# The adaLN sums over rows: 32x32 block transposes and additions on VectorE, and a fold of 8 columns on TensorE

## The chip, the cores and the metric

One core of a Trainium2 chip runs the whole program. The time is that of the device for one execution, in microseconds; the core has TensorE (matrix products), VectorE, ScalarE and GpSimd (work on rows), and DMA queues that bring the weights from HBM.

## The reference

Two layers of a transformer trunk over 256 latent and 256 context tokens with 1024 features. Each layer is a half-step FFN, a mixing stage and a second half-step FFN; the norm ahead of each, and the result of each, are modulated by nine vectors of 1024 values. These come from the conditioning vectors `c` and `c_ctx` through one matrix per layer:

```python
def modulate(h, shift, scale):
    return h * (1 + scale) + shift

def ffn_half_step(h, shift, scale, gate, g, w_in, w_out):
    a, b = jnp.split(modulate(rms_norm(h, g), shift, scale) @ w_in, 2, axis=-1)
    return h + FFN_RESIDUAL_WEIGHT * gate * ((jax.nn.silu(a) * b) @ w_out)
...
    sc, scc = jax.nn.silu(c), jax.nn.silu(c_ctx)
    for l in range(DEPTH):
        mod_l = jnp.split((sc @ w_ada[l] + b_ada[l])[:, None, :], ADA_CHUNKS, axis=-1)
        mod_c = jnp.split((scc @ w_ada[l] + b_ada[l])[None, None, :], ADA_CHUNKS, axis=-1)
        h = ffn_half_step(h, mod_l[0], mod_l[1], mod_l[2], g_ffn1[l], w_ffn1_in[l], w_ffn1_out[l])
        hc = ffn_half_step(hc, mod_c[0], mod_c[1], mod_c[2], g_ffn1[l], w_ffn1_in[l], w_ffn1_out[l])
```

The change concerns only the product `sc @ w_ada[l]` and its twin for the context: two vectors of 1024 times a 1024 x 9216 matrix, per layer.

## The kernel before

The stream `h` lies feature by feature: 8 blocks of 128 features on the partitions, 512 tokens in the columns. Weights come as tiles `raw` of 128 x 1024 through SyncE's DMA queue, in the order of use, six tiles ahead (class `Weights`). ScalarE copies each into a high part `whi` (L125), VectorE (or GpSimd) takes the rest as a low part `wlo` (L126), five weights ahead of their use; both are written into the buffer of a weight that TensorE has finished. A product of 128 x 128 weights with 512 tokens is three matmuls, high by high, high by low and low by high (L384 to L386).

The work is a list of jobs, emitted one after the other; each engine keeps its instructions in the order of emission. An FFN has 22 pairs of blocks: `pair_a` and `pair_b` are 24 matmuls each, after which `evac` forms silu(a) times b (ScalarE L452, VectorE L453, ScalarE L454, VectorE L455). Then come 8 output blocks of three jobs (8, 8 and 6 blocks of 128 features, three matmuls each, 66 in all).

The adaLN products are spread between these jobs. `ada_job` puts one tile of `w_ada` (256 rows by 512 columns of one of the chunks) after a job: in the first FFN after both jobs of each of its 19 later pairs and after two jobs of each of the first five output blocks, in the two FFNs around the layers' boundary less densely. VectorE multiplies its rows by the two conditioning values of each partition and adds them up in `scratch`, four instructions of 128 x 512 per tile (L276 for the first two of a sum, L278 otherwise). Four tiles (part 0 to 3) make one sum, half a chunk: 512 columns for two streams, with 128 partial sums each, one per partition. `scratch` is one buffer of 128 x 1024.

The addition over the partitions then goes through TensorE. `pend` is a list of emissions with a count of ordinary jobs by which they come later. `ada_sum` (count 2) multiplies the four quarters of `scratch` by ones, each into another group of 32 rows of a PSUM bank `sm` (L288, two passes each); ScalarE copies the result (L291). `ada_finish` (count 1, from there) transposes it back on TensorE, so that features lie on partitions (L297), and VectorE adds the bias (L304). `sm` has two buffers.

Of the kernel before, what the change touches and what calls it, by code (L numbers as in the profile page):

```python
# [8 lines left out]
F32 = mybir.dt.float32  # L9
# [6 lines left out]
L = 2  # L16
# [23 lines left out]
# packed per-partition parameters: name -> columns for one layer  # L40
# [20 lines left out]
class Weights:  # L61
    """Streams weights in order: DRAM -> raw tile -> (high, low) float32r parts, ahead of their use.
    SPARE in the stream is room of one weight, left to other uses between its take and its done."""
# [29 lines left out]
    def pump(self, preps=None):  # L93
        """Start the loads that have room, and prepare the parts (at most preps, when held back)."""
        nc = self.nc
        go = True
        left = preps if preps is not None else (0 if self.hold else 1 << 30)
        while go:
            go = False
            while self.dma_i < len(self.raws) and self.dma_i < self.raw_pref + RAWB:  # L100
                raw = self.raws[self.dma_i]
                t = self.pool.tile([128, RAWN], F32, tag="raw", name="raw", bufs=RAWB)
                nc.sync.dma_start(out=t[:, 0:raw["n"]], in_=raw["ap"])
                self.raw_t[self.dma_i] = t
                self.dma_i += 1
                go = True
            while left > 0 and self.prep_i < len(self.subs) and self.prep_i < self.sub_pref + SUBB:
                if self.subs[self.prep_i] is None:
                    self.sub_t[self.prep_i] = self._parts(F32)
                    self.prep_i += 1  # L110
                    left -= 1
                    continue
                r, (off, n, gains) = self.subs[self.prep_i]
                if r >= self.dma_i:
                    break
                left -= 1
                eng = nc.gpsimd if self.low == "g" or (self.low == "a" and self.prep_i % 2) else nc.vector
                t = self.raw_t[r]
                hi, lo = self._parts()
                step = n // len(gains)  # L120
                for i, g in enumerate(gains):
                    a, b = i * step, (i + 1) * step
                    src = t[:, off + a:off + b]
                    if g is None:
                        nc.scalar.activation(hi[:, a:b], src, AF.Copy)  # L125
                        eng.tensor_tensor(lo[:, a:b], src, hi[:, a:b].bitcast(F32), ALU.subtract)  # L126
                    else:
                        nc.scalar.activation(hi[:, a:b], src, AF.Copy, scale=g())
                        nc.vector.scalar_tensor_tensor(
                            lo[:, a:b], src, g(), hi[:, a:b].bitcast(F32), ALU.mult, ALU.subtract)  # L130
                self.sub_t[self.prep_i] = (hi, lo)
                self.prep_i += 1
                self.raw_left[r] -= 1
                if self.raw_left[r] == 0:
                    self._raw_done(r)
                go = True
# [38 lines left out]
def hybrid_trunk_kernel(ctx: ExitStack, tc: tile.TileContext, io: dict, out: bass.AP):  # L175
# [13 lines left out]
    scr = cp.tile([128, 1], F32, name="scr")  # L189
    cs = cp.tile([128, DK, 32], F32, name="cs")  # L190
# [31 lines left out]
    def new_scratch():  # L222
        """4 KB that hold either sums of the adaLN products or the pieces of a norm"""
        t = tp.tile([128, 4, 256], F32, tag="scratch", name="scratch", bufs=1)
        st["scr"], st["scr_u"], st["scr_d"] = t, 0, 0
        return t
# [14 lines left out]
    # ---------------------------------------------------------------- weight specs  # L241
# [16 lines left out]
    # ---------------------------------------------------------------- adaLN  # L258
    pend = []

    def ada_tile(l, c, t):
        """Products of 2 x 128 rows and 512 columns of one chunk, summed over row blocks on VectorE."""
        half, part = divmod(t, 4)

        def fn(W):
# [14 lines left out]
            if part == 3:  # L280
                a = st["ada"]
                pend.append([2, lambda: ada_sum(l, c, half, a)])
        return fn

    def ada_sum(l, c, half, acc):
        bank = sm_bank()
        for g in range(4):
            PE.matmul(bank[32 * g:32 * g + 32, 0:256], lhsT=ones[:, 0:32], rhs=acc[:, g], start=True, stop=True,  # L288
                      skip_group_check=True)
        sb = temp(512, "sa", 2)  # L290
        ACT.activation(sb[:, 0:256], bank[:, 0:256], AF.Copy)  # L291
        pend.append([1, lambda: ada_finish(l, c, half, sb)])

    def ada_finish(l, c, half, sb):
        trb = sm_bank()
        for e in range(2):
            PE.transpose(trb[:, 128 * e:128 * e + 128], sb[:, 128 * e:128 * e + 128], ident)  # L297
        v = trb[:, 0:256].rearrange("p (e s q m) -> p s q e m", e=2, s=2, q=2)[:, :, :, :, 0]
# [3 lines left out]
        bias = vec[:, l, o + 8 * c + 4 * half:o + 8 * c + 4 * half + 4].rearrange("p (q e) -> p q e", q=2)  # L302
        bias = bias.unsqueeze(1).broadcast_to([128, 2, 2, 2])
        DVE.tensor_tensor(m.rearrange("p (q e) s -> p s q e", q=2), v, bias, ALU.add)  # L304
# [17 lines left out]
    # ---------------------------------------------------------------- norms over features  # L322
    def stats(acc, sl, n):
        """diagonals of the rstd of each token of sl, from squares summed over blocks in acc."""
        fin = stats_a(acc, sl, n)
        return fin()
# [25 lines left out]
    def split_norm(src, dst_h, dst_l, rb, a, b=None, eng=None):  # L352
        """high and low parts of src * a * rb (+ b); returns the emission of the low part."""
# [17 lines left out]
    def staggered(makers):  # L371
        """runs emissions that return a follow-up, each follow-up one later"""
# [20 lines left out]
    # ---------------------------------------------------------------- residual update  # L393
    def resid(l, gc, j, bank, half, first, last_use=False):
        """h += gate * bank, and its squares into the accumulator of the next norm."""
# [17 lines left out]
    # A norm chain for the halves of the stream, cut in steps that are emitted between other work.  # L413
    def chain(l, i, half):
        """generator: each next() emits one step; the steps use PE, ACT and DVE."""
# [17 lines left out]
    # ---------------------------------------------------------------- FFN  # L433
    def ffn(l, which, ntok, tail, first=None):
        """tail(part): called by the last block to start the chain of what follows."""
# [28 lines left out]
        def first_two(W):  # L464
            """Blocks 0 and 1: the latent half while the norm of the context half is under way."""
# [147 lines left out]
    def boundary(l, i):  # L613
        """tail of the last block before norm i of layer l: work(0..2) is the ctx half in three parts."""
# [18 lines left out]
    # ---------------------------------------------------------------- mixing  # L633
    def mixing(l):
# [35 lines left out]
        def tok_part(banks, subs, k0, n, tiles, W=None):  # L670
            """banks[t] += x[:, tile t] of the rows in subs; frees the weights when W is given"""
# [41 lines left out]
        def lat_tr(names, nk, dh, dl, gain):  # L713
            """transposed normalised latents, times their gains, into dh/dl"""
# [16 lines left out]
        # kv latents  # L731
# [49 lines left out]
        def k_prep(W):  # L781
            """shared rope part of the keys: squares, gains, rotation"""
            kpe = P["kpe"]
            # rope tables with the heads' gains
# [66 lines left out]
        # short gated conv, feature-major; blocks c, x, b per 128 channels  # L851
# [38 lines left out]
        # spatial gating: weights loaded whole, transposed by the host  # L890
# [30 lines left out]
        def y_sg(W):  # L921
            """transposed gated features into y blocks 4, 5"""
# [25 lines left out]
        # up-projections, token-major  # L948
# [110 lines left out]
        # attention  # L1059
# [9 lines left out]
        def A(n):  # L1069
            """transposed queries and keys of a head; returns the emissions of the high and the low parts"""  # L1070
# [22 lines left out]
        def B(n, lows):  # L1093
            """scores and their exponentials; lows are emissions of other work, after the maxima"""
# [52 lines left out]
        def C(n):  # L1147
            """transposed probabilities; returns the emissions of their evacuation"""
# [23 lines left out]
        def Dv(j, s, bk):  # L1172
            """probabilities times values of heads 2j and 2j+1, side by side on the array, for one half of the
            queries; returns the emissions of the evacuation and of the squares"""
# [73 lines left out]
        # output projection  # L1248
# [84 lines left out]
    # ---------------------------------------------------------------- program  # L1333
# [3 lines left out]
    def init(W):  # L1337
# [7 lines left out]
        make_identity(nc, ident)  # L1345
        DVE.memset(cs, 0.0)
# [37 lines left out]
    def first_blocks(in_spec, evac, half_mm):  # L1384
        """Blocks 0 to 2 of the first FFN: feature by feature, as the modulation of each becomes known."""
# [103 lines left out]
    # order of the weight stream: the adaLN tiles, which wait for their use in place, come a little later  # L1489
# [29 lines left out]
def _layout(i):  # L1519
# [4 lines left out]
    def cols(v):  # L1524
        """[L, n*128] -> [128, L, n]"""
# [3 lines left out]
    def blocks(w, n):  # L1529
        """[L, K*128, N] -> [L, N/n, 128, K, n]"""  # L1530
# [3 lines left out]
    def flat(w):  # L1534
        """[L, K*128, N] -> [L, 128, K*N]"""
# [77 lines left out]
```

## Time and profile before

| | |
|---|---|
| time, median of 3 runs | 1779.28 us (1777.94 to 1781.04) |
| span of the profiled execution, first to last instruction | 1778.8 us |
| its own time beside the span | not listed apart; the span is 0.5 us below the median of the runs |
| TensorE, matmuls | 1715.4 us busy, 96% |
| VectorE | 1077.7 us busy, 61% |
| ScalarE | 661.1 us busy, 37% |
| GpSimd | 328.9 us busy, 18% |
| DMA | 248.59 MB, mean 140 GB/s |

The shares of busy time are averages over stages: FFNs, in which matmuls follow one another without a gap, and the mixing stages, in which the engines wait for one another in turn. What a change is worth has to be read in the stage where it runs. A busy TensorE is one that has a matmul under way; matmuls are pipelined, so what one costs is the distance of two starts, not its length.

### The profile page before, as it was taken

How to read it: one execution, taken by the hardware profiler on the slowest of the kernel's cores; microseconds unless marked ns; L12 is line 12 of the kernel's file. 1: busy time of each engine (PE TensorE's matmuls, PEld its weight loads, DVE VectorE, ACT ScalarE, POOL GpSimd, SP SyncE). 2: the span in 40 equal slices, each digit the busy share in tenths (PEclk: the TensorE clock that was granted, in tenths of full speed). 3: DMA queues.
4: the chain of work that ended last, by engine and by line, in shares of the span. 5: the costliest groups of instructions: out<-in, count | busy, mean ns of one | idle time of the engine just before them, and what ended most of it. 6: DMA issues, size and time to landing. Idle time of an engine off the chain costs nothing.

```text
span 1778.8 us, 24162 instructions
## 1 busy us (share of the span) xinstructions
PE 1715.4 (96%) x9422; PEld 1450.0 (82%) x9422; DVE 1077.7 (61%) x1778; ACT 661.1 (37%) x1124; POOL 328.9 (18%) x210
## 2 busy tenths in 40 slices
PE   8999999999998999999999999999999987889999
PEld 6888888889876688888888888888888986589999
DVE  5667777635578475575766356576765577554332
ACT  4422223224457443222232242222222355554442
POOL 0000000004346522000000030000000165465442
PEclk9999999999999999999999999999999998899999
DMA  8545555523211124454555234454454242136553
GB/s 318 189 158 181 184 182 191 178 84 98 82 60 48 37 70 151 134 176 155 165 175 166 98 107 158 162 164 161 158 174 123 70 142 69 36 116 210 185 180 94
DMA packets 71395, 248.59 MB, mean 140 GB/s; under 512 B 8048, under 2 KB 9584, under 8 KB 71280
## 3 DMA queue, kind: packets, MB, share of 16 engines
q1 hardware_dynamic: 71136, 246.97, 42.3%
q8 instruction: 74, 1.21, 0.3%
q14 instruction: 41, 0.34, 0.1%
q10 hardware_dynamic: 144, 0.07, 0.0%
HBM read 245.96 MB, written 1.05 MB: 139 GB/s over the span
## 4 chain that ended last, share of the span: by engine, by line
PE 87%; DVE 7%; ACT 3%; issue 2%; POOL 1%; DMA 1%; ACTq 0%; POOLq 0%; DVEq 0%
PE mm L384 26%; PE mm L385 25%; PE mm L386 25%; PE mm L389 2%; PE mm L391 2%; PE mm L390 2%; PE sm L288 1%; ACT p L1130 1%; PE sm L1181 1%; DVE mx L1119 1%; PE mm L1363 1%; DMA raw<-in_w_ada 1%; DVE xl L361 1%; PE sm L1076 1%; PE mm L1158 1%
## 5 line engine op out<-in xcount | busy, mean ns | idle before, releaser
L384 PE MATMUL mm<-xh,whi 128*128 128x512 f32 (+1 forms) x1712 | 612.0, 358 | 6.5 <-DVE kvl L723 3.1
L385 PE MATMUL mm<-xl,whi 128*128 128x512 f32 (+1 forms) x1712 | 605.7, 354 | 4.0 <-DVE xl L361 3.4
L386 PE MATMUL mm<-xh,wlo 128*128 128x512 f32 (+1 forms) x1712 | 604.1, 353 | 1.8 <-POOL wlo L126 1.3
L125 ACT ACTIVATE whi<-raw 128x1024 fp32r<-128x1024 f32 (+1 forms) x334 | 339.1, 1020 | 486.3 <-PE mm L385 373.6
L126 POOL TENSOR_TENSOR wlo<-raw,whi 128x1024 fp32r<-128x1024 f32 (+3 forms) x112 | 258.1, 2318 | 1335.7 <-ACT whi L125 1320.3
L126 DVE TENSOR_TENSOR wlo<-raw,whi 128x1024 fp32r<-128x1024 f32 (+2 forms) x222 | 265.9, 1199 | 244.8 <-ACT whi L125 244.8
L384 PEld LDWEIGHTS mm<-xh,whi 128*128 128x128 f32 x1712 | 327.4, 191 | 63.9 <-issue 11.8
L385 PEld LDWEIGHTS mm<-xl,whi 128*128 128x128 f32 x1712 | 327.4, 191 | 48.2 <-DVE xl L361 4.5
L386 PEld LDWEIGHTS mm<-xh,wlo 128*128 128x128 f32 x1712 | 327.4, 191 | 45.6 <-POOL wlo L126 1.5
L278 DVE SCALAR_TENSOR_TENSOR scratch<-raw,cs,scratch 128x512 f32<-128x512 f32 x448 | 307.4, 745 | 0.0
L384 PE MATMUL mm<-gh,whi 128*128 128x512 f32 (+1 forms) x770 | 270.2, 351 | 0.0
L386 PE MATMUL mm<-gh,wlo 128*128 128x512 f32 (+1 forms) x770 | 267.1, 347 | 0.0
L385 PE MATMUL mm<-gl,whi 128*128 128x512 f32 (+1 forms) x770 | 267.0, 347 | 0.0
L454 ACT ACTIVATE gh<-sa 128x512 fp32r<-128x512 f32 (+1 forms) x88 | 50.9, 579 | 310.2 <-DVE sa L453 310.2
L384 PEld LDWEIGHTS mm<-gh,whi 128*128 128x128 f32 x770 | 145.8, 189 | 22.3 <-issue 4.9
L386 PEld LDWEIGHTS mm<-gh,wlo 128*128 128x128 f32 x770 | 145.8, 189 | 18.3
L385 PEld LDWEIGHTS mm<-gl,whi 128*128 128x128 f32 x770 | 145.9, 189 | 17.5
L276 DVE TENSOR_SCALAR scratch<-raw,cs 128x512 f32<-128x512 f32 x64 | 28.2, 484 | 148.9 <-PE sm L288 148.9
L455 DVE TENSOR_TENSOR gl<-sa,gh 128x512 fp32r<-128x512 f32 (+1 forms) x88 | 57.7, 656 | 56.8 <-ACT gh L454 56.8
L453 DVE TENSOR_TENSOR sa<-sa,mm 128x512 f32<-128x512 f32 (+1 forms) x88 | 53.9, 613 | 17.7 <-PE mm L386 16.0
L408 DVE TENSOR_TENSOR acc<-acc,sq 128x256 f32<-128x256 f32 x63 | 41.4, 657 | 35.1 <-ACT sq L407 35.1
L360 ACT ACTIVATE xh<-scratch,mods 128x256 fp32r<-128x256 f32 x88 | 42.8, 506 | 52.9 <-DVE scratch L356 52.9
(207 smaller groups left out, 1457.6 us busy)
## 6 DMA issues: line engine op xcount, KB each, us to landing
raw<-in_w_ffn_in SPq DMA_DIRECT2D x176, 512.0 KB, 3.9
raw<-in_w_ada SPq DMA_DIRECT2D x144, 512.0 KB, 4.2
raw<-in_w_ffn_out SPq DMA_DIRECT2D x64, 512.0 KB, 4.4
raw<-in_w_ffn_out SPq DMA_DIRECT2D x32, 384.0 KB, 3.4
raw<-in_w_mo SPq DMA_DIRECT2D x16, 512.0 KB, 3.5
raw<-in_w_cv SPq DMA_DIRECT2D x12, 512.0 KB, 3.7
raw<-in_w_uv SPq DMA_DIRECT2D x8, 512.0 KB, 3.9
raw<-in_w_q SPq DMA_DIRECT2D x8, 384.0 KB, 3.1
```

The costliest lines, as they stand in the source:

```text
L125: nc.scalar.activation(hi[:, a:b], src, AF.Copy)
L126: eng.tensor_tensor(lo[:, a:b], src, hi[:, a:b].bitcast(F32), ALU.subtract)
L278: DVE.scalar_tensor_tensor(acc[:, s], src, cv, acc[:, s], ALU.mult, ALU.add)
L360: ACT.activation(dst_h, u, AF.Identity, bias=b)
L384: PE.matmul(bank, lhsT=wh, rhs=xh, start=first, stop=False)
L385: PE.matmul(bank, lhsT=wh, rhs=xl, start=False, stop=False)
L386: PE.matmul(bank, lhsT=wl, rhs=xh, start=False, stop=last)
L389: PE.matmul(bank, lhsT=xh, rhs=wh, start=first, stop=False)
L408: DVE.tensor_tensor(acc[:, half], acc[:, half], sq, ALU.add)
L453: DVE.tensor_tensor(sa[:, 0:n], sa[:, 0:n], bb[:, 0:n], ALU.mult)
L454: ACT.activation(st["gh"][:, m, 0:n], sa[:, 0:n], AF.Copy)
L455: DVE.tensor_tensor(st["gl"][:, m, 0:n], sa[:, 0:n], st["gh"][:, m, 0:n].bitcast(F32), ALU.subtract)
```

## The change

The products and their sums in `scratch` stay. Right behind the last products of a sum, in the same job, VectorE transposes each stream's 128 x 512 partial sums in blocks of 32 x 32 from `scratch` into a bank `sm`, and adds along each run of 32 columns, which leaves 16 values per partition and stream in `red`. What is left of the addition is over the four groups of 32 partitions: four matmuls of 8 columns with `fold`, a 128 x 32 matrix of four identities under one another, each into another group of 32 rows of a bank. Features then lie on partitions, so the ones, ScalarE's copy and TensorE's transposes are gone. `ada_sum` no longer goes through `pend`; `ada_finish`, which now holds the fold, has the count 1. `fold` is formed once, at the start, from the identity.

```diff
+    fold = cp.tile([128, 32], F32, name="fold")
...
             if part == 3:
-                a = st["ada"]
-                pend.append([2, lambda: ada_sum(l, c, half, a)])
+                ada_sum(l, c, half, st["ada"])
         return fn
 
     def ada_sum(l, c, half, acc):
+
+        a = acc[:, :, :].rearrange("p (s q) n -> p s (q n)", s=2)
+        red = temp(32, "red", 2)
+        for s in range(2):
+            t = sm_bank()
+            DVE.transpose(t, a[:, s])
+            DVE.tensor_reduce(red[:, 16 * s:16 * s + 16], t[:, :].rearrange("p (b i) -> p b i", i=32), AX.X, ALU.add)
+        pend.append([1, lambda: ada_finish(l, c, half, red)])
+
+    def ada_finish(l, c, half, red):
+
         bank = sm_bank()
+        v = red[:, :].rearrange("p (s k g) -> p g s k", s=2, g=4)
         for g in range(4):
-            PE.matmul(bank[32 * g:32 * g + 32, 0:256], lhsT=ones[:, 0:32], rhs=acc[:, g], start=True, stop=True,
+            PE.matmul(bank[32 * g:32 * g + 32, 0:8], lhsT=fold, rhs=v[:, g], start=True, stop=True,
                       skip_group_check=True)
-        sb = temp(512, "sa", 2)
-        ACT.activation(sb[:, 0:256], bank[:, 0:256], AF.Copy)
-        pend.append([1, lambda: ada_finish(l, c, half, sb)])
-
-    def ada_finish(l, c, half, sb):
-        trb = sm_bank()
-        for e in range(2):
-            PE.transpose(trb[:, 128 * e:128 * e + 128], sb[:, 128 * e:128 * e + 128], ident)
...
+        DVE.tensor_reduce(fold, ident[:, :].rearrange("p (r j) -> p j r", r=4), AX.X, ALU.add)
```

The lines of the changed kernel are numbered two to five higher than those of before: its products are L277 and L279, its matmuls L386 to L388.

On VectorE, around the end of the first sum of the first FFN, the last products (L278) stood straight ahead of the next weight's low part and the next sum's first products:

```order
L453 TENSOR_TENSOR sa<-sa,mm 128x512
L455 TENSOR_TENSOR gl<-sa,gh 128x512
L278 SCALAR_TENSOR_TENSOR scratch<-raw,cs,scratch 128x512 x4
L126 TENSOR_TENSOR wlo<-raw,whi 128x1024
L276 TENSOR_SCALAR scratch<-raw,cs 128x512 x2
```

Now, at the same place, with the addition of the bias two jobs later:

```order
L455 TENSOR_TENSOR sa<-sa,mm 128x512
L457 TENSOR_TENSOR gl<-sa,gh 128x512
L279 SCALAR_TENSOR_TENSOR scratch<-raw,cs,scratch 128x512 x4
L291 STREAM_TRANSPOSE sm<-scratch 128x512
L292 TENSOR_REDUCE red<-sm 128x16
L291 STREAM_TRANSPOSE sm<-scratch 128x512
L292 TENSOR_REDUCE red<-sm 128x16
L126 TENSOR_TENSOR wlo<-raw,whi 128x1024
L277 TENSOR_SCALAR scratch<-raw,cs 128x512 x2
L279 SCALAR_TENSOR_TENSOR scratch<-raw,cs,scratch 128x512 x2
L126 TENSOR_TENSOR wlo<-raw,whi 128x1024
L455 TENSOR_TENSOR sa<-sa,mm 128x512
L457 TENSOR_TENSOR gl<-sa,gh 128x512
L306 TENSOR_TENSOR mods<-sm,vec 128x2x4
```

Four instructions now stand between the last products and what follows them, and the next sum's first products follow the reader of `scratch` on the same engine.

On TensorE, the same sum stood three jobs behind the last products, and its transposes two jobs behind that:

```order
L386 MATMUL mm<-xh,wlo 128x512
L288 MATMUL sm<-scratch,ones 32x256 x4
L384 MATMUL mm<-xh,whi 128x512
...
L386 MATMUL mm<-xh,wlo 128x512
L297 MATMUL sm<-ident,sa 128x128 x2
L384 MATMUL mm<-xh,whi 128x512
```

Now the fold is the only one of these, 24 matmuls (one job) ahead of where the sum was:

```order
L387 MATMUL mm<-xl,whi 128x512
L388 MATMUL mm<-xh,wlo 128x512
L300 MATMUL sm<-red,fold 32x8 x4
L386 MATMUL mm<-xh,whi 128x512
L387 MATMUL mm<-xl,whi 128x512
```

TensorE's queue has one interruption per sum where it had two.

## Rows read from the trace of the kernel before

**Rows 1.** The page: busy time of each engine, and the chain by engine.
```profile
PE 1715.4 (96%) x9422; PEld 1450.0 (82%) x9422; DVE 1077.7 (61%) x1778; ACT 661.1 (37%) x1124; POOL 328.9 (18%) x210
...
PE 87%; DVE 7%; ACT 3%; issue 2%; POOL 1%; DMA 1%; ACTq 0%; POOLq 0%; DVEq 0%
```

**Rows 2.** Stretches from sum to sum: length, busy time, TensorE's clock, DMA, GB/s.
```profile
194.60:217.41 22.81, 22.81 (x111) 18.27 (x114) 17.35 (x25) 6.53 (x9) 0.00 (x0) 1.00 0.55 183
...
338.28:369.25 30.97, 30.97 (x146) 25.03 (x150) 20.15 (x31) 7.88 (x12) 0.00 (x0) 1.00 0.50 149
...
753.47:781.72 28.25, 28.25 (x134) 22.78 (x138) 18.74 (x27) 8.04 (x11) 0.00 (x0) 1.00 0.51 168
```

**Rows 3.** VectorE's instructions by line and shape: busy, mean ns, idle before.
```profile
L276 DVE TENSOR_SCALAR scratch<-raw,cs 128x512 f32<-128x512 f32 x64 | 28.2, 484 | 148.9 <-PE sm L288 148.9
L1119 DVE TENSOR_REDUCE mx<-mm 128x1 f32<-128x512 f32 x32 | 21.1, 684 | 6.9 <-PE mm L391 6.8
...
L1166 DVE COPY pt<-mm 128x512 f32<-128x512 f32 x12 | 8.1, 674 | 6.4 <-PE sm L1181 4.3 <-PE mm L1158 2.1
...
L877 DVE SCALAR_TENSOR_TENSOR vtmp<-z,vec,vtmp 128x512 f32<-128x512 f32 x2 | 5.5, 2774 | 0.1
```

**Rows 4.** Order in time, TensorE around one sum: start, length, instruction.
```profile
213.63 0.39 PE L386 MATMUL mm<-xh,wlo 128*128 128x512 f32 x1
...
217.03 0.39 PE L386 MATMUL mm<-xh,wlo 128*128 128x512 f32 x1
217.34 0.64 PE L288 MATMUL sm<-scratch,ones 128*32 128x256 f32 x8
217.91 0.50 PE L384 MATMUL mm<-xh,whi 128*128 128x512 f32 x1
...
218.25 0.39 PE L385 MATMUL mm<-xl,whi 128*128 128x512 f32 x1
```

**Rows 5.** Order in time, TensorE around the transposes of the sum.
```profile
228.71 0.39 PE L386 MATMUL mm<-xh,wlo 128*128 128x512 f32 x1
...
228.94 0.38 PE L297 MATMUL sm<-ident,sa 128*128 128x128 f32 x2
...
229.07 0.48 PE L384 MATMUL mm<-xh,whi 128*128 128x512 f32 x1
...
229.39 0.39 PE L385 MATMUL mm<-xl,whi 128*128 128x512 f32 x1
```

**Rows 6.** The sum's two batches in narrow windows, and its weight loads (min/median/max ns).
```profile
217.34 0.42 PE L288 MATMUL sm<-scratch,ones 128*32 128x256 f32 x4
...
217.58 0.40 PE L288 MATMUL sm<-scratch,ones 128*32 128x256 f32 x4
...
L288 PEld LDWEIGHTS sm<-scratch,ones x256: 106/108/109, 103.3 to 1366.6; 128*32 128x32 f32 x128
```

**Rows 7.** ScalarE's copy of the sum, by line: busy, mean ns.
```profile
L291 ACT ACTIVATE sa<-sm 128x256 f32<-128x256 f32 x32 | 11.7, 366 | 0.0
```

**Rows 8.** Order in time around the last products of the first sum.
```profile
86.89 1.06 ACT L125 ACTIVATE whi<-raw 128x1024 fp32r<-128x1024 f32 x1 [4.42 <-PE mm L385]
...
91.11 2.73 DVE L278 SCALAR_TENSOR_TENSOR scratch<-raw,cs,scratch 128x512 f32<-128x512 f32 x4
...
97.77 1.06 ACT L125 ACTIVATE whi<-raw 128x1024 fp32r<-128x1024 f32 x1 [4.43 <-PE mm L385]
...
103.99 0.88 DVE L276 TENSOR_SCALAR scratch<-raw,cs 128x512 f32<-128x512 f32 x2 [9.01 <-PE sm L288]
```

**Rows 9.** VectorE's wait at the first products of a later sum.
```profile
218.05 0.88 DVE L276 TENSOR_SCALAR scratch<-raw,cs 128x512 f32<-128x512 f32 x2 [4.06 <-PE sm L288]
```

**Rows 10.** The start of the program: the identity, and the memset and activation of cs.
```profile
1.00 0.27 DVE L1346 MEMSET cs<- 128x256 f32 x1
1.01 0.29 POOL masks.py:199 TENSOR_SCALAR_AFFINE_SELECT ident<-ident 128x128 f32<-128x128 f32 x1
...
2.48 0.22 ACT L1349 ACTIVATE cs<-craw 128x16 f32<-128x16 f32 x1 [0.25 <-DMA craw<-in_cc]
```

More of the change, by code (lines that the diff above doesn't have):

```diff
@@ L280, in fn @@
             if part == 3:
-                a = st["ada"]
-                pend.append([2, lambda: ada_sum(l, c, half, a)])
+                ada_sum(l, c, half, st["ada"])
         return fn
     def ada_sum(l, c, half, acc):
+        a = acc[:, :, :].rearrange("p (s q) n -> p s (q n)", s=2)
[6 more added lines that the diff above has]
+    def ada_finish(l, c, half, red):
         bank = sm_bank()
+        v = red[:, :].rearrange("p (s k g) -> p g s k", s=2, g=4)
         for g in range(4):
-            PE.matmul(bank[32 * g:32 * g + 32, 0:256], lhsT=ones[:, 0:32], rhs=acc[:, g], start=True, stop=True,
+            PE.matmul(bank[32 * g:32 * g + 32, 0:8], lhsT=fold, rhs=v[:, g], start=True, stop=True,
                       skip_group_check=True)
-        sb = temp(512, "sa", 2)
-        ACT.activation(sb[:, 0:256], bank[:, 0:256], AF.Copy)
-        pend.append([1, lambda: ada_finish(l, c, half, sb)])
-    def ada_finish(l, c, half, sb):
-        trb = sm_bank()
-        for e in range(2):
-            PE.transpose(trb[:, 128 * e:128 * e + 128], sb[:, 128 * e:128 * e + 128], ident)
-        v = trb[:, 0:256].rearrange("p (e s q m) -> p s q e m", e=2, s=2, q=2)[:, :, :, :, 0]
         ks = slice(4 * half, 4 * half + 4)
@@ L301, in ada_finish @@
         o, _ = VOFF["b_ada"]
-        bias = vec[:, l, o + 8 * c + 4 * half:o + 8 * c + 4 * half + 4].rearrange("p (q e) -> p q e", q=2)
-        bias = bias.unsqueeze(1).broadcast_to([128, 2, 2, 2])
-        DVE.tensor_tensor(m.rearrange("p (q e) s -> p s q e", q=2), v, bias, ALU.add)
+        bias = vec[:, l, o + 8 * c + 4 * half:o + 8 * c + 4 * half + 4].unsqueeze(1).broadcast_to([128, 2, 4])
+        DVE.tensor_tensor(m.rearrange("p k s -> p s k"), bank[:, 0:8].rearrange("p (s k) -> p s k", s=2), bias, ALU.add)
         if c in (1, 4, 7):
```

## The prediction

> **What bounds the kernel now.** I read the page's busy shares and its chain of work first, then the stretches between two sums of adaLN products, then the groups of instructions by line, then the order in time. TensorE is busy 96% of the span and holds 87% of the chain that ended last [rows 1]; VectorE has 61%. The averages hide that the kernel has two kinds of stage, so I looked at the stretches in which the changed code runs: from one sum (line 288) to the next in the first FFN's pairs, in its output part, and in a later FFN. In all three TensorE is busy for the whole stretch, at a granted clock of 1.00 (the 2.4 GHz level), while VectorE has idle time [rows 2]. A microsecond taken from TensorE's queue there is a microsecond of the end, as long as nothing that TensorE needs comes late. VectorE's largest wait there is at line 276: 148.9 us in all, for TensorE's sums to give back the one scratch tile; the 64 instructions of that line, two per sum, say that there are 32 sums [rows 3]. That wait delays nobody on the chain, so its removal is worth nothing by itself. It is room for new work.
>
> **What the change takes from TensorE.** In the pairs fifteen matmuls of 512 columns start between 213.63 and 217.03 us, so one costs 0.2267 us [rows 4]. Between two sums lie 4 jobs of 24 matmuls, 96 x 0.2267 = 21.76 us, and the stretch is 22.81 long: 1.05 us belong to one sum. The same comes out of the output part (132 matmuls, 29.92 of 30.97) and of the later FFN (120 matmuls, 27.20 of 28.25) [rows 2]. All sums together are 32 x 1.05 = 33.6 us of the span, the most that this change can take away.
>
> Where the 1.05 goes: the L386 ahead of the sum starts at 217.03 and the L385 after it at 218.25, where two pitches would be 0.45, so the sum costs 1.22 - 0.45 = 0.77 [rows 4]. The two transposes cost (229.39 - 228.71) - 0.45 = 0.23 [rows 5]. About 0.05 is left in the matmuls behind them, which run a little off their pitch.
>
> The transposes go: 0.23. The sum's matmuls stay, four into four column groups, but with 8 columns for 256. What that is worth is the uncertain term. The eight instructions (two passes of four) run in two batches: four start together at 217.34, the second four by 217.58, 0.24 later, and the last of these is 0.40 long; the next full-width matmul starts at 217.91, 0.07 before that end [rows 6, 4]. So the group is 0.24 + 0.40 - 0.07 = 0.57 long, and around it lie 0.77 - 0.57 = 0.20 of going over to column groups and back, which I keep. Of the 0.40, about 0.21 is the streaming of 256 columns (the 0.24 between batches less 0.03 of starts); with 8 columns 0.20 is left. The distance of the batches is bounded above by today's 0.24, below by one load of 32 columns, 0.108 [rows 6]. The group becomes 0.11 to 0.24, plus 0.20 - 0.07: 0.24 to 0.37. I take the middle, 0.30, since neither the load nor the stream is plainly the limit. The new cost is 0.20 + 0.30 and half of the 0.05, 0.53; the saving per sum is 1.05 - 0.53 = 0.52 (0.43 to 0.59 at the ends), and 32 x 0.52 = **16.6 us** (13.8 to 18.9).
>
> **What it takes from ScalarE.** One copy of 0.37 us per sum [rows 7]. ScalarE isn't on the chain in these stretches, so nothing.
>
> **What it adds to VectorE.** Per sum two transposes of 128x512 from SBUF into PSUM and two reductions of 128x512 out of PSUM. A reduction of that size takes 0.68 us; a transpose isn't in the trace. From below a 128x512 instruction with one operand takes 0.48 (line 276), a copy with one side in PSUM 0.67, and the slowest 128x512 instruction of any kind is 2.77 [rows 3]. I take 0.68, since the copy has the same operands: 4 x 0.68 = 2.7 us per sum, bounds 2.3 and 6.9. The Trainium skill ("VectorE: DVE Perf Modes", The three transpose paths) gives 311 ns for a VectorE transpose of 128x128 bf16; scaled by column it would be an estimate of some 0.7 us here and the sum 2.8, but no run here shows it. The same page (Rules for kernel authors) calls the reduction the slowest VectorE instruction and advises against it on a hot path; the row agrees, 0.68 against 0.48 for the same size, and if this were VectorE-bound the rule would decide against the change.
>
> Is it? The tightest stage is the pairs of the first FFN, with an adaLN tile after every job. A stretch there is 22.81 long and VectorE's only long wait in it is 4.06 for the sum [rows 2, 9], so its own work, with its short waits for ScalarE, is 18.75. TensorE's new stretch is 22.81 - 0.52 = 22.29. Room: 22.29 - 18.75 = 3.5 against 2.7. VectorE keeps up with 0.8 to spare, and its bound falls only if the four instructions exceed 3.5 us.
>
> The second question is when TensorE needs the result. Before, the sum stands three jobs behind the last products, now the fold stands two behind. The first sum shows VectorE when it isn't held back. The job before the last products ended when ScalarE's weight copy was let go, at 86.89; the last products start at 91.11 and last 2.73, until 93.84. The second job after it ends at 97.77 (the copy let go by TensorE again) [rows 8]. That leaves 3.9 us, and 2.7 go to the new instructions: ready 1.2 us before TensorE arrives. The scratch tile is then free at once, where VectorE now waits 9.01 us for it at 103.99 [rows 8], so the later stretches start no later than this one. VectorE's add behind the fold is queued after that pair's evacuation and comes later than the fold; it waits for nothing. Both small PSUM banks are now used by the transposes, in an order in which the previous sum's add has long passed. Weights and output banks are prepared several jobs ahead, so 2.7 us of work in place of 4.06 us of waiting makes none of them later.
>
> **At the start** a reduction of the identity stands ahead of the memset of cs in VectorE's queue. The identity is done at 1.30; at most 0.68 for the reduction (the 128x512 one, four times as large [rows 3]) and 0.27 for the memset end by 2.25, and the activation that needs cs starts at 2.48, after its load [rows 10]. Nothing; without that cover it would be at most 0.7 us.
>
> **Sum.** The profiled span is 1778.8 us, 0.5 below the median of the runs, 1779.28; I carry the difference over. 1779.3 - 16.6 = **1762.7 us**, 0.9% faster. A change of 0.2%, 3.6 us, is about what a measurement of this kernel can tell from none.
>
> **Rivals.**
> *The columns don't matter.* The fold costs what the sum did, because going to column groups and back, with two batches of loads, sets the 0.57. Then only the transposes and half of the 0.05 go: 32 x 0.255 = 8.2 us, **1771.1**. For it: the 0.20 around the group is no streaming, and the distance of the batches could be its loads. Against it: the two batches are as far apart as their columns take. The Trainium skill ("TensorEngine Tiling (Array Packing)", Key Properties) says that a change of the tiling mode drains TensorE; the 0.20 that I keep agrees with it, and by that rule taken as the whole cost this rival would hold. Chance 0.14.
> *VectorE takes what TensorE gives.* The four instructions cost 3.5 to 4.6, for instance since a reduction must wait for the end of its transpose. VectorE then falls behind at the 9 sums of the pairs of the first FFN (19 pairs, 38 tiles, four to a sum), and past 3.9 TensorE also waits at folds elsewhere. With 9 x (x - 3.5) + 11.5 x (x - 3.9) (half of the other 23 taken as tight) the saving is used up at x = 4.6. **1763 to 1780**. Chance 0.06, half of it within 0.2% of no change. This is also the case in which the change doesn't do what it says.
> *The transpose is slow, and the kernel becomes slower.* At 2.77 each, x = 6.9: 9 x 3.4 + 11.5 x 3.0 = 65 us of waits at the fold against 16.6 saved, about **1828**. It decides from x = 4.6, a transpose of 1.6 us, more than twice the copy. Against it: only instructions in the mixing stage, on lines unlike this, take that long. Chance 0.07.
> *The switch goes too.* With so short a group nearly the whole 1.05 vanishes: 33 us, **1746**. Against it: the gaps at either side of the group. Chance 0.03.
>
> **How the numbers follow.** My forecast has 0.70, with a range of its own of 1759 to 1766. The whole range, 1757 to 1772, takes in the first rival and part of the second, and leaves out somewhat over one in ten. Faster by over 0.2%: 0.70 + 0.14 + 0.03 + 0.03 = 0.90; within 0.2%: 0.03; slower: 0.07.
>
> **What the next profile would show.** Right: stretches of the first FFN's pairs of about 22.3 us with TensorE busy throughout, no row of TensorE waiting for VectorE's reduction, no wait at the first products, transposes and reductions near 0.7 us, the fold's group near 0.3 long. Wrong: TensorE idle ahead of the fold (slow VectorE), stretches of 22.55 (columns don't matter), or weight parts that come late behind VectorE.

## The result, and the profile after

| | before | after |
|---|---|---|
| median of 4 runs each, us | 1778.8 (1777.94 to 1781.04) | 1757.88 (1757.77 to 1763.03) |
| span of the profiled execution, us | 1778.8 | 1756.0 |
| that execution's own time, us | not listed apart | 1757.77 |

The ratio is 0.9889, with a 95% interval of 0.987 to 0.9907: 20.9 us less, where 16.6 were forecast. The 1757.88 us lie within the whole range of the prediction, 1757 to 1772, by 0.9 us, and below the range of its own forecast, 1759 to 1766.

The page of the changed kernel, its busy times and the chain by engine, which answer to [rows 1]:

```profile
PE 1696.6 (97%) x9358; PEld 1444.0 (82%) x9358; DVE 1162.4 (66%) x1907; ACT 655.8 (37%) x1092; POOL 328.9 (19%) x210
...
PE 86%; DVE 8%; ACT 3%; issue 2%; POOL 1%; DMA 0%; ACTq 0%; POOLq 0%; DVEq 0%
```

TensorE is still the bound. VectorE is busy 85 us more and the span is 22.8 us shorter, so the added work is hidden.

A stretch from one fold to the next in the first FFN's pairs (length, busy time of TensorE, its weight loads, VectorE, ScalarE, GpSimd, then the granted clock, DMA share and GB/s), which answers to the first of [rows 2]:

```profile
99.44:121.61 22.17, 22.17 (x105) 18.10 (x105) 20.16 (x31) 6.49 (x9) 0.00 (x0) 1.00 0.60 190
```

22.17 us against 22.81, with TensorE busy throughout and VectorE's busy time up from 17.35 to 20.16. 0.64 us per sum times 32 is 20.5 us, about the 20.9 of the medians. The two spans differ by 2.3 us more. Most of that is the choice of the execution: the changed kernel's time is 1.8 us above its span, and with the same 1.8 the profiled execution of the kernel before took an estimated 1780.6 us, 1.8 above its median.

The order in time on TensorE around one fold, which answers to [rows 4]:

```profile
99.13 0.39 PE L388 MATMUL mm<-xh,wlo 128*128 128x512 f32 x1
99.44 0.25 PE L300 MATMUL sm<-red,fold 128*32 128x8 f32 x8
99.62 0.50 PE L386 MATMUL mm<-xh,whi 128*128 128x512 f32 x1
99.96 0.39 PE L387 MATMUL mm<-xl,whi 128*128 128x512 f32 x1
```

From the L388 ahead to the L387 behind it are 0.83 us, where two pitches are 0.45: the fold costs 0.38. Its group is 99.62 - 99.44 = 0.18 long; the old sum's was 0.57. Read in the same way, each of the 32 folds in this trace costs 0.38 and each of the 32 sums in the trace before 0.77, so the one shown stands for all.

VectorE at the same place in the program, and the weight copies of ScalarE that TensorE lets go at the end of the job before the last products and of the second one behind it (both from the order in time); they answer to [rows 8]:

```profile
88.50 1.06 ACT L125 ACTIVATE whi<-raw 128x1024 fp32r<-128x1024 f32 x1 [4.43 <-PE mm L387]
...
95.37 0.72 DVE L291 STREAM_TRANSPOSE sm<-scratch 128x512 f32<-128x512 f32 x1
96.12 0.69 DVE L292 TENSOR_REDUCE red<-sm 128x16 f32<-128x512 f32 x1
96.73 0.72 DVE L291 STREAM_TRANSPOSE sm<-scratch 128x512 f32<-128x512 f32 x1
97.48 0.69 DVE L292 TENSOR_REDUCE red<-sm 128x16 f32<-128x512 f32 x1
98.09 1.22 DVE L126 TENSOR_TENSOR wlo<-raw,whi 128x1024 fp32r<-128x1024 f32 x1
99.22 0.88 DVE L277 TENSOR_SCALAR scratch<-raw,cs 128x512 f32<-128x512 f32 x2
...
99.37 1.06 ACT L125 ACTIVATE whi<-raw 128x1024 fp32r<-128x1024 f32 x1 [4.42 <-PE mm L387]
```

The four new instructions take 98.09 - 95.37 = 2.72 us. Each reduction starts after the end of its transpose (96.12 against 96.09), and the second transpose and the next weight's low part start 0.08 us before the end of the reduction ahead of them. The last ends at 98.17, 1.2 us before TensorE lets the second copy go at 99.37 and comes to the fold. The next sum's first products follow without a wait, where [rows 8] had 9.01.

### The profile page after: what moved, and what is told of

It is laid out like the page before. It is cut to its first block, busy times and chain, and to the rows that moved or that the text cites. A ratio compares the mean times of both kernels' runs of the same rounds, so it can differ in the third digit from the quotient of the medians.

```text
span 1756.0 us, 24072 instructions
## 1 busy us (share of the span) xinstructions
PE 1696.6 (97%) x9358; PEld 1444.0 (82%) x9358; DVE 1162.4 (66%) x1907; ACT 655.8 (37%) x1092; POOL 328.9 (19%) x210
## 4 chain that ended last, share of the span: by engine, by line
PE 86%; DVE 8%; ACT 3%; issue 2%; POOL 1%; DMA 0%; ACTq 0%; POOLq 0%; DVEq 0%
PE mm L386 26%; PE mm L387 25%; PE mm L388 25%; PE mm L393 2%; PE mm L391 2%; PE mm L392 2%; DVE xl L363 1%; ACT p L1132 1%; DVE mx L1121 1%; PE sm L1183 1%; PE mm L1366 1%; DVE scratch L358 1%; PE sm L1078 0%; DVE vtmp L879 0%; DVE vtmp L878 0%
## 5 line engine op out<-in xcount | busy, mean ns | idle before, releaser
L386 PE MATMUL mm<-xh,whi 128*128 128x512 f32 (+1 forms) x1712 | 611.2, 357 | 6.3 <-DVE kvl L725 3.1
L387 PE MATMUL mm<-xl,whi 128*128 128x512 f32 (+1 forms) x1712 | 607.0, 355 | 4.2 <-DVE xl L363 4.2
L388 PE MATMUL mm<-xh,wlo 128*128 128x512 f32 (+1 forms) x1712 | 605.0, 353 | 1.8 <-POOL wlo L126 1.3
L386 PEld LDWEIGHTS mm<-xh,whi 128*128 128x128 f32 x1712 | 328.1, 192 | 57.7 <-ACT xh L360 4.9
L387 PEld LDWEIGHTS mm<-xl,whi 128*128 128x128 f32 x1712 | 327.9, 192 | 49.8 <-DVE xl L363 5.9
L388 PEld LDWEIGHTS mm<-xh,wlo 128*128 128x128 f32 x1712 | 328.1, 192 | 45.1 <-POOL wlo L126 1.5
L279 DVE SCALAR_TENSOR_TENSOR scratch<-raw,cs,scratch 128x512 f32<-128x512 f32 x448 | 307.4, 745 | 0.0
L386 PE MATMUL mm<-gh,whi 128*128 128x512 f32 (+1 forms) x770 | 268.8, 349 | 0.0
L388 PE MATMUL mm<-gh,wlo 128*128 128x512 f32 (+1 forms) x770 | 267.0, 347 | 0.0
L387 PE MATMUL mm<-gl,whi 128*128 128x512 f32 (+1 forms) x770 | 266.9, 347 | 0.0
L386 PEld LDWEIGHTS mm<-gh,whi 128*128 128x128 f32 x770 | 145.8, 189 | 18.1
L388 PEld LDWEIGHTS mm<-gh,wlo 128*128 128x128 f32 x770 | 145.8, 189 | 18.1
L387 PEld LDWEIGHTS mm<-gl,whi 128*128 128x128 f32 x770 | 145.8, 189 | 18.0
L409 ACT ACTIVATE sq<-h 128x256 f32<-128x256 f32 x63 | 26.2, 416 | 104.7 <-DVE h L401 104.7
```

Source lines behind the costliest of these rows:

```text
L279: DVE.scalar_tensor_tensor(acc[:, s], src, cv, acc[:, s], ALU.mult, ALU.add)
L386: PE.matmul(bank, lhsT=wh, rhs=xh, start=first, stop=False)
L387: PE.matmul(bank, lhsT=wh, rhs=xl, start=False, stop=False)
L388: PE.matmul(bank, lhsT=wl, rhs=xh, start=False, stop=last)
```

## The experiments

Changes are against the changed kernel unless said otherwise. Ratios are to the kernel before, in the same session.

### What the fold and the transposes cost TensorE

**Two transposes back.**

```diff
         if c in (2, 8):
             DVE.tensor_scalar(m, m, 0.5, None, ALU.mult)
+        pend.append([1, two_transposes])
+
+    def two_transposes():
+        trb = sm_bank()
+        for e in range(2):
+            PE.transpose(trb[:, 128 * e:128 * e + 128], ident, ident)
```

> The changed kernel with the two TensorE transposes of before put back at their old place, two jobs behind the fold, on the identity and into a bank that nobody reads. Theory: each pair of them costs 0.23 us of TensorE, 32 x 0.23 = 7.4 us, so about 1765. Rival (the transposes were hidden in the pitch of the matmuls, or cost their 0.38 us of busy time): 1758, or 1770.

1767.26 us, ratio 0.9935 (0.992 to 0.995), 9.4 us above the changed kernel. The interval is 1764 to 1769.5 and holds the 1765. The order in time of this run shows the same price as [rows 5], (110.39 - 109.71) - 0.45 = 0.23:

```profile
109.71 0.39 PE L394 MATMUL mm<-xh,wlo 128*128 128x512 f32 x1
109.94 0.38 PE L318 MATMUL sm<-ident 128*128 128x128 f32 x2
110.08 0.48 PE L392 MATMUL mm<-xh,whi 128*128 128x512 f32 x1
110.39 0.39 PE L393 MATMUL mm<-xl,whi 128*128 128x512 f32 x1
```

**The fold with 256 columns.**

```diff
-            PE.matmul(bank[32 * g:32 * g + 32, 0:8], lhsT=fold, rhs=v[:, g], start=True, stop=True,
-                      skip_group_check=True)
+            PE.matmul(bank[32 * g:32 * g + 32, 0:256], lhsT=fold,
+                      rhs=red[:, :].rearrange("p (n g) -> p g n", g=4)[:, g:g + 1, :].broadcast_to([128, 32, 8]),
+                      start=True, stop=True, skip_group_check=True)
```

> The changed kernel, but each of the four fold matmuls moves 256 columns (the same 8 repeated 32 times) in place of 8, so the result and every wait stay. Theory (the saving of the fold is TensorE's streaming of columns): the group becomes as long as the old sum's, 0.57 us for 0.18, so 32 x 0.39 = 12.5 us come back and the time is about 1770. Rival (the columns don't matter, the saving of the fold comes from its place or from the scratch tile set free early): 1758, as the changed kernel.

1790.02 us, ratio 1.0051 (1.0035 to 1.0068): 32 us above the changed kernel, and above the kernel before, which has the transposes too. The columns matter, so the rival falls, but the size expected was too small by a factor of more than two. The order in time of this run:

```profile
97.81 0.39 PE L389 MATMUL mm<-xh,wlo 128*128 128x512 f32 x1
98.13 1.10 PE L300 MATMUL sm<-red,fold 128*32 128x256 f32 x8
99.16 0.50 PE L387 MATMUL mm<-xh,whi 128*128 128x512 f32 x1
```

The group is 1.03 us long, not 0.57; 32 x (1.03 - 0.18) is 27 us, to 1785, which is where the interval, 1784.6 to 1790.5, begins. The other 5 us aren't accounted for; the mean granted clock of the profiled execution was 0.977 here and 0.982 in the changed kernel. What differs from the old sum is how its operand is read: every fourth value of `red`, and the same eight again and again. Two runs take these apart.

**256 columns, read in a row.**

```diff
-            DVE.tensor_reduce(red[:, 16 * s:16 * s + 16], t[:, :].rearrange("p (b i) -> p b i", i=32), AX.X, ALU.add)
+            DVE.tensor_reduce(red[:, :].rearrange("p (g s k) -> p s k g", g=4, s=2)[:, s],
+                              t[:, :].rearrange("p (k g i) -> p k g i", g=4, i=32), AX.X, ALU.add)
...
-            PE.matmul(bank[32 * g:32 * g + 32, 0:8], lhsT=fold, rhs=v[:, g], start=True, stop=True,
-                      skip_group_check=True)
+            PE.matmul(bank[32 * g:32 * g + 32, 0:256], lhsT=fold,
+                      rhs=red[:, 8 * g:8 * g + 8].unsqueeze(1).broadcast_to([128, 32, 8]),
+                      start=True, stop=True, skip_group_check=True)
```

> As the run with 256 columns in the fold, but the 8 values of a group lie side by side in red (the reduction writes them so), so each matmul reads runs of 8 neighbours, where that run reads every fourth value. Theory (the group there was 1.05 us long, not 0.57, since TensorE streams every fourth 4-byte value at half speed): 0.57 us again, 32 x 0.39 = 12.5 us above the changed kernel, about 1770. Rival (the slowing comes from four groups reading the same few addresses over and over): 1785 to 1790, as in that run.

**The kernel before, reading every fourth value** (against before).

```diff
-            PE.matmul(bank[32 * g:32 * g + 32, 0:256], lhsT=ones[:, 0:32], rhs=acc[:, g], start=True, stop=True,
-                      skip_group_check=True)
+            PE.matmul(bank[32 * g:32 * g + 32, 0:256], lhsT=ones[:, 0:32],
+                      rhs=acc[:, :, :].rearrange("p a n -> p (a n)").rearrange("p (n g) -> p g n", g=4)[:, g],
+                      start=True, stop=True, skip_group_check=True)
```

> The kernel before, but its sum's four matmuls read every fourth value of scratch in place of 256 neighbours; the sums land in other columns than they belong to, so this run changes what is computed. Theory (every fourth value streams at half speed): the sum's group grows from 0.57 to 1.05 us, 32 x 0.48 = 15 us, about 1794. Rival (the step between values is free): 1779.

The first took 1773.61 us (ratio 0.9964, 0.995 to 0.9978: 1770 to 1775), the second 1793.6 (1.0086, 1.0065 to 1.0107: 1790.5 to 1798). The theory's 1770 lies at the edge of the first interval, its 1794 in the middle of the second; the rivals' 1785 to 1790 and 1779 lie outside. The order in time, first of the fold in a row, then of the kernel before with its step of four:

```profile
97.64 0.39 PE L389 MATMUL mm<-xh,wlo 128*128 128x512 f32 x1
97.95 0.64 PE L300 MATMUL sm<-red,fold 128*32 128x256 f32 x8
98.53 0.50 PE L387 MATMUL mm<-xh,whi 128*128 128x512 f32 x1
98.86 0.40 PE L388 MATMUL mm<-xl,whi 128*128 128x512 f32 x1
```

```profile
102.60 0.39 PE L387 MATMUL mm<-xh,wlo 128*128 128x512 f32 x1
102.92 1.09 PE L288 MATMUL sm<-scratch,ones 128*32 128x256 f32 x8
103.94 0.50 PE L385 MATMUL mm<-xh,whi 128*128 128x512 f32 x1
```

In a row the group is 0.58 long and the fold costs 1.22 - 0.45 = 0.77, which is the old sum's cost in [rows 4]. With a step of four the group of the old sum grows to 1.02. So the shrinking from 256 columns to 8 is worth 0.77 - 0.38 = 0.39 us per sum, 12.5 us of the span; the rest of the run with 256 columns, 32 x (1.03 - 0.58) = 14 us, was its own way of reading.

### Where VectorE's work hides, and when it stops

**The kernel before, its sum one job earlier** (against before).

```diff
-                pend.append([2, lambda: ada_sum(l, c, half, a)])
+                pend.append([1, lambda: ada_sum(l, c, half, a)])
```

> The kernel before, with its sum emitted two jobs behind the last products in place of three, so that the scratch tile comes free one job (5.4 us) earlier and most of VectorE's 148.9 us of waiting goes, while TensorE's work stays the same. Theory (that wait delayed nobody on the chain): no change, 1779. Rival (part of the saving came from ending that wait, through earlier weight parts and loads): faster, up to some 6 us.

1779.0 us, ratio 1.0 (0.9988 to 1.0012). VectorE's wait at line 276 falls from 148.9 us to this, by the waits of that line:

```profile
  PE sm L288: 55.5, 17
```

93 us of VectorE's waiting are gone, and the time is the same to within 2 us. To that accuracy the scratch tile set free early is no part of the gain.

**Half more, and twice the work on VectorE.** The diff is that of half more; the other has `range(2)`.

```diff
-            DVE.transpose(t, a[:, s])
-            DVE.tensor_reduce(red[:, 16 * s:16 * s + 16], t[:, :].rearrange("p (b i) -> p b i", i=32), AX.X, ALU.add)
+            for _ in range(2 - s):
+                DVE.transpose(t, a[:, s])
+                DVE.tensor_reduce(red[:, 16 * s:16 * s + 16], t[:, :].rearrange("p (b i) -> p b i", i=32), AX.X, ALU.add)
```

> The changed kernel with the transpose and the reduction of the first stream done twice: 4.08 us of VectorE per sum in place of 2.72. Theory (hidden up to the room of 22.17 - 18.75 = 3.4 us in the pairs of the first FFN and up to 3.9 us ahead of the fold elsewhere; beyond that TensorE waits): 9 x 0.66 + 11.5 x 0.18 = 8 us, about 1766. Rivals: all of VectorE's work is on the path, 32 x 1.36 = 44 us, 1801; or nothing of it is, since weights are prepared five ahead, 1758.

> The changed kernel with both transposes and both reductions done twice: 5.44 us of VectorE per sum. Theory: 9 x 2.0 + 11.5 x 1.5 = 36 us, about 1794, slower than before: the point at which the change turns into a loss lies between this run and the one with 4.08 us. Rivals: all on the path, 32 x 2.72 = 87 us, 1845; or still hidden, 1758.

1767.7 us (0.994, 0.9919 to 0.9961) and 1803.94 us (1.0138, 1.0112 to 1.0164), so 9.8 and 46 us above the changed kernel. TensorE's waits for the reduction, the largest group of its waits, of the run with half more and then of the run with twice the work (us in total, times, longest):

```profile
PE sm L301 <- DVE red L293: 7.0, 13, 0.8
```

```profile
PE sm L301 <- DVE red L293: 35.2, 22, 2.3
```

8 and 36 us were worked out, 7.0 and 35.2 are there. They also lie where the theory put them: 5.8 and 17.6 us at the nine sums of the first FFN's pairs (9 x 0.66 = 5.9 and 9 x 2.0 = 18 expected), the rest elsewhere. The changed kernel itself has no such row. That twice the work costs more than 36 is taken up in the next run.

**The fold one job earlier.**

```diff
-        pend.append([1, lambda: ada_finish(l, c, half, red)])
+        pend.append([0, lambda: ada_finish(l, c, half, red)])
```

> The changed kernel with the fold emitted one job behind the last products in place of two, 5.4 us earlier in TensorE's queue. Theory (TensorE waits for the reduction where it isn't ready): the result is ready 9.7 us after the end of the job before the products (8.0 where that job is the first of a pair), and TensorE now comes at 5.4, so it waits 4.2 us at 9 sums of the first FFN's pairs and 2.6 to 4.2 at the other 23: 1856 to 1893. Rival (the result is there early, or TensorE's queue has slack): 1758.

1931.97 us, ratio 1.0865 (1.0847 to 1.0884): 174 us above the changed kernel, where 98 to 135 were expected. TensorE's waits, then its order in time around one of them, then stretches ahead of it and behind it (the last three figures of a stretch are the granted clock, the DMA share and GB/s):

```profile
PE sm L300 <- DVE red L292: 111.1, 32, 4.2
```

```profile
91.94 0.39 PE L388 MATMUL mm<-xh,wlo 128*128 128x512 f32 x1
96.57 0.25 PE L300 MATMUL sm<-red,fold 128*32 128x8 f32 x8 [4.24 <-DVE red L292]
...
98.27 0.63 PE L387 MATMUL mm<-xl,whi 128*128 128x512 f32 x1
98.70 0.63 PE L388 MATMUL mm<-xh,wlo 128*128 128x512 f32 x1
```

```profile
85.00:92.00 7.00, 7.00 (x33) 5.73 (x31) 5.07 (x8) 2.18 (x3) 0.00 (x0) 1.00 0.78 243
...
97.20:100.50 3.30, 3.30 (x10) 2.55 (x9) 2.71 (x7) 0.00 (x0) 0.00 (x0) 0.50 0.53 151
...
101.00:103.00 2.00, 2.00 (x10) 1.66 (x9) 0.00 (x0) 0.00 (x0) 0.00 (x0) 1.00 0.70 236
```

The waits are those of the theory: 4.24 us here where 4.2 were expected, 32 of them, 111 in all. The other 63 us come after them. Behind this wait the granted clock falls to 0.50 for some us, 1.2 for 2.4 GHz, and two starts are 0.43 us apart where they are 0.2267 otherwise. It falls behind every one of the 32 waits: in the 5 us behind each the time at half clock adds up to 124 us, and half of that, 62 us, is lost. The run with twice the work has the same behind three of its 22 waits only, of 1.8 to 2.3 us, and not behind others of the same length. Here are the stretches behind its first three waits, of 1.78, 1.78 and 2.33 us:

```profile
100.90:104.10 3.20, 3.20 (x9) 2.49 (x8) 3.20 (x6) 0.00 (x0) 0.00 (x0) 0.50 0.56 157
126.00:130.00 4.00, 4.00 (x18) 3.31 (x19) 4.00 (x7) 0.00 (x0) 0.00 (x0) 1.00 0.48 139
150.60:154.60 4.00, 4.00 (x18) 3.31 (x19) 4.00 (x7) 0.00 (x0) 0.00 (x0) 1.00 0.45 133
```

Three such stretches cost an estimated 3 x 1.6 = 5 us (3.2 us at half the clock each). The profiled execution of that run has a span of 1798.0 us, 42.0 above the changed kernel's: 35.2 of waits and these 5 make up most of it. The remaining 4 of the 46 are the distance of that execution, 1799.82 us, from the median of its four.

### A version that beats both

**One fold per chunk.** The two halves of a chunk leave their sums side by side, and only the second calls the fold; the bias, gain and half follow for all eight blocks of features at once.

```diff
-        red = temp(32, "red", 2)
+        if half == 0:
+            st["red"] = temp(64, "red", 2)
+        red = st["red"]
...
-        pend.append([1, lambda: ada_finish(l, c, half, red)])
+        if half == 1:
+            pend.append([1, lambda: ada_finish(l, c, red)])
...
-            PE.matmul(bank[32 * g:32 * g + 32, 0:8], lhsT=fold, rhs=v[:, g], start=True, stop=True,
+            PE.matmul(bank[32 * g:32 * g + 32, 0:16], lhsT=fold, rhs=v[:, g], start=True, stop=True,
```

> The changed kernel with one fold for the two halves of a chunk: 16 groups of four matmuls of 16 columns in place of 32 of 8. Theory (what is left of a sum on TensorE, 22.17 - 21.76 = 0.41 us, is going over to column groups and back, and hardly depends on the columns): 16 x 0.41 = 6.6 us less, about 1751. Rival (what is left belongs to the columns or to waits): 1758.

**And with a full-width fold.** `full` is four copies of `fold` side by side, `grp` a mask of 128 x 4 that is one where a partition belongs to the row group.

```diff
...
+        PE.matmul(bank[:, 0:64], lhsT=full, rhs=red, start=True, stop=True)
+        own, one = bank[:, 64:128], bank[:, 128:144]
+        DVE.tensor_tensor(own.rearrange("p (n g) -> p n g", g=4), bank[:, 0:64].rearrange("p (n g) -> p n g", g=4),
+                          grp[:, :].unsqueeze(1).broadcast_to([128, 16, 4]), ALU.mult)
+        DVE.tensor_reduce(one, own.rearrange("p (n g) -> p n g", g=4), AX.X, ALU.add)
...
```

> As the run with one fold per chunk, but the fold is one matmul of 64 columns with a full 128 x 128 matrix of identities (two passes), and VectorE keeps each row group's own columns by a mask and one more addition. Theory (the 0.20 us around the group is the change to column groups and back, which a full-width matmul doesn't make): a group costs 0.23 us, what the two full-width transposes cost, to 0.43, so 13.1 - 16 x (0.23 to 0.43) = 6 to 9 us less than the changed kernel, 1749 to 1752, and at least as fast as the run with column groups. Rival (the narrow groups are not what costs, a 128-column load is dearer): slower than the run with column groups.

1753.25 us (0.9852, 0.9836 to 0.9868) and 1750.73 us (0.9835, 0.9819 to 0.9852). Against the changed kernel that is 4.6 and 7.2 us less, measured in another session; the first interval ends just below where the changed kernel's begins (0.9868 and 0.987), and the two overlap each other, so that the second is the better of the two isn't shown by the times; the order in time speaks for it. The fold of 16 columns, then the full-width one:

```profile
119.98 0.39 PE L392 MATMUL mm<-xh,wlo 128*128 128x512 f32 x1
120.30 0.26 PE L304 MATMUL sm<-red,fold 128*32 128x16 f32 x8
...
120.83 0.39 PE L391 MATMUL mm<-xl,whi 128*128 128x512 f32 x1
```

```profile
119.61 0.40 PE L394 MATMUL mm<-xh,wlo 128*128 128x512 f32 x1
119.85 0.33 PE L303 MATMUL sm<-red,full 128*128 128x64 f32 x2
...
120.30 0.39 PE L393 MATMUL mm<-xl,whi 128*128 128x512 f32 x1
```

0.85 - 0.45 = 0.40 us for twice the columns in column groups, about the 0.38 of 8: half as many folds cost about half. The full-width one costs 0.69 - 0.45 = 0.24, as the two transposes did. The Trainium skill ("TensorEngine Tiling (Array Packing)", Key Properties) says that changing the tiling mode drains TensorE; the trace is in line with it, in that eight short matmuls with two such changes cost 0.40 and two full-width ones without cost 0.24. It doesn't show the drain by itself, since the two also differ in the number and the width of their matmuls and loads.

## Why the prediction was right, and where its size was off

- **The number.** The forecast was 1762.7 us, with 1759 to 1766 of its own; the time, 1757.88, lies below that, between the forecast and the rival in which the switch goes too. That the whole range still holds it, by 0.9 us, is partly luck: its lower end wasn't worked out from a term.
- **The bound.** A microsecond of TensorE's queue is one of the end, and VectorE's wait for the scratch tile is none. Shown: 0.64 us less per stretch with TensorE busy throughout, times 32, against 20.9 measured; and the run that took 93 us of that wait away, with a ratio of 1.0.
- **The transposes**, 0.23 per sum. Shown, by putting them back.
- **The fold's group**, 0.30 long (0.24 to 0.37). This is the term that was off: it is 0.18. The step that failed is the lower bound of the distance of the two batches, one load of 32 columns, 0.108. Here are the lengths of the fold's loads and matmuls in the changed kernel (ns, min/median/max), and the eight loads of one fold in the order of time (start, length of all):

```profile
L300 PEld LDWEIGHTS sm<-red,fold x256: 106/108/109, 99.4 to 1341.2; 128*32 128x32 f32 x128
L300 PE MATMUL sm<-red,fold x256: 176/186/197, 99.4 to 1341.2; 128*32 128x8 f32 x128
...
99.44 0.16 PEld L300 LDWEIGHTS sm<-red,fold 128*32 128x32 f32 x8 [0.35 <-PE mm L387]
```

Each load is as long as before (106 to 109 ns), but all eight lie within 0.16 us, so they overlap, and eight matmuls of 0.186 lie within 0.25 us, so their starts within about 0.06. The trace of the kernel before had shown the overlap already:

```profile
217.34 0.16 PEld L288 LDWEIGHTS sm<-scratch,ones 128*32 128x32 f32 x8 [0.35 <-PE mm L385]
```

There the loads of both batches were over at 217.50, and the second batch was at work by 217.58. So the length of one load was no bound at all; with the same eight loads and 8 columns for 256 the starts move together, so what set the batches 0.24 apart was their columns. 0.06 + 0.19 - 0.07 is 0.18. That is 0.12 per sum less than forecast, 3.8 of the 4.3 us by which the forecast saving was too small. Everything around the group (0.20) stayed as forecast, 0.38 - 0.18.
- **VectorE's price**, 2.7 us per sum from the copy's row. Measured 2.72: transposes of 0.72, reductions of 0.69. That the transpose came so near is in part luck: the copy reads PSUM and writes SBUF, the transpose the other way round. The prediction's 0.7 and 2.8 don't follow from the figure of the Trainium skill ("VectorE: DVE Perf Modes", The three transpose paths) that they are given with: scaled by the columns, 311 ns make 4 x 0.311 = 1.24 us and an estimate of 2 x (1.24 + 0.68) = 3.8 for the sum, over the room of 3.5. The measured 0.72 is far below that. The prediction also reads its rows as agreeing that the reduction is the slowest instruction of VectorE. They don't: [rows 3] itself has one of 2.77 us, and the multiply-and-add of L278 took 0.745 us in that trace, the reduction 0.684.
- **The room and the slack.** 3.5 us of room (3.4 with the shorter stretch) and 1.2 us ahead of the fold. The slack is in the trace as forecast, at the first sum; at none of the 32 does TensorE wait. The room is shown by the two runs with more work, whose waits came out within 1 us of what was worked out.
- **The rival that ends on the other side** is real and its point is bracketed: 4.08 us of VectorE per sum still gains, 5.44 loses, and a straight line between the two times meets the kernel before at 4.5. The prediction says 4.6; its own sum, 9 x (x - 3.5) + 11.5 x (x - 3.9) = 16.6, gives 4.5. Its price beyond that was too low: the clock behind longer waits wasn't in it (5 us of 42 at x = 5.44; 62 of 174 with the fold one job earlier).
- **The columns don't matter:** refuted, 0.39 us per sum between 8 columns and 256 in a row.

## What to carry to other kernels

Where one engine is the bound, cost a small insertion by the distance of the starts around it, less the pitch, and not by its busy time; the sum of these over all insertions is the most that a change there can give. An engine with waiting time can take work over, but only what fits between the input's arrival and the moment the bound engine needs the result; work out both in the tightest stage, and add the clock's fall to the price of missing it. If small results can wait, gather them, and do the rest in the array shape of the matmuls around it (here 0.24 us for 0.40).

## What the runs showed of the hardware that wasn't expected

- TensorE streams every fourth 4-byte value of an operand at about half the rate of neighbours: 256 such columns in four column groups made a group of 1.02 to 1.03 us in two different kernels, 0.57 to 0.58 in a row; over the 0.18 of 8 columns that is 0.85 against 0.40. Reading the same eight values over and over costs nothing (0.58 against 0.57 for 256 different ones).
- All 32 waits of 2.1 to 4.2 us in one run's otherwise dense stretches of TensorE were followed by a granted clock of 0.50 for some us, and 111 us of waits cost 174 in all. In another run it fell behind 3 of 22 waits of up to 2.3 us, and behind 13 waits of up to 0.8 us in a third not at all. What decides this for a wait of about 2 us no run here shows.
- Eight matmuls of 8 columns in four column groups, in two passes, start within about 0.06 us, although each load lasts 0.108: the eight loads overlap and lie within 0.16 us.
